# A decoder layer on one core: V's first gathers one per chunk, the zero fill from a small tile and earlier, norm sums and the overflow count later

## The chip, the cores and the metric

The kernel runs on 1 core of one Trainium2 chip (trn2). The metric is the device time of one execution in microseconds (us). The inputs are in the chip's memory before the start, and the kernel is one launch. The engines have separate instruction queues: TensorE (PE in the profile, with its weight loads as PEld), VectorE (DVE), ScalarE (ACT), GpSimd (POOL) and SyncE (SP, which here only issues DMAs). Each queue runs its instructions in order. An instruction that waits holds all that stand behind it on its engine.

## The reference, cut to what matters

One layer of a decoder in float32, for 256 tokens of width 2048, and a last RMSNorm:

```
def hybrid_layer(h, mem, ...):
    hn = rmsnorm(h, norm_mix)
    q_nsa, k_cmp, v_cmp, k_slc, v_slc, k_win, v_win, gate_logits, q_sb, k_sb, v_sb = split(hn @ w_in)
    o_nsa = nsa_attention(q_nsa, ..., t5_table)              # 8 heads, compressed + selected + window
    o_sb = stick_breaking_attention(q_sb, k_sb, v_sb)        # 8 heads
    h = h + concat(o_nsa, o_sb) @ w_out
    h = h + memory_attention(rmsnorm(h, norm_mem_q), rmsnorm(mem, norm_mem_kv), ...)   # 4 heads, 256 memory tokens
    h = h + peer_ffn(rmsnorm(h, norm_ffn), peer_w_q, peer_sub_keys, peer_u, peer_v)
    return h

def peer_ffn(hn, w_pq, sub_keys, u_tab, v_tab):              # per token: 8 heads x 16 experts of 16384
    q = hn @ w_pq                                            # two half queries of 128 per head
    s = q . sub_keys ; top_s, top_i = top_k(s, 16)           # per half: 128 keys, the best 16
    best_s, best_c = top_k(top_s[0] + top_s[1], 16)          # of 256 pairs the best 16
    expert = ia * 128 + ib ; gate = softmax(best_s)
    a = hn . u_tab[expert] ; hidden = gate * gelu(a)
    return sum over the experts of hidden * v_tab[expert]
```

## The kernel before, in words

**Products.** Every float32 product is made of float32r parts. A weight tile of 512 KB (128 x 1024) is loaded by SP into a `raw` buffer (four of them, L60 to L63). ACT copies it into `hi` (L71) and DVE subtracts to get `lo` (L73); there are three buffers of each. A *half block* is one such tile: eight matmuls with `hi` against a pair of activations (L89, 512 columns) and eight with `lo` (L91, 256 columns). Two half blocks make a block of 128 output columns (`fm_block`). `self.last_lo` is always the latest instruction that made a `lo`.

**Stages, in order.** (1) Memory values and keys and the norm of `x`. POOL sums squares (`square_sum`, L183 to L189) into `ssq_m` and `ssq_x`. PE adds these up over the partitions with a matrix of ones (L174 `ps_ssq`, L396 `ps_col`), and ACT and DVE make the reciprocal roots of them (`rstd_rows`, `rstd_columns`). (2) `w_kv`, `w_q`, `w_v`, and four calls of `nsa`, each of which ends with `out_pair` (L578). (3) `w_vsb`, then eight heads of stick-breaking attention; each head makes its `q` and `k` (`qk`), which POOL multiplies by `rstd` (L338). (4) `w_out` in 16 blocks, and memory attention. (5) PEER: 16 blocks of `w_pq`, the two top-16 searches cut into `pieces`, then the *U loop*: all 16384 rows of U as 128 *chunks* of 128 experts, each a block of two half blocks. (6) The *V phase*: rows of V, gathered by expert number, in five calls of `run`. (7) The last norm, in two halves of the tokens.

**The gate table and the lists.** The gates of the chosen experts are scattered into a table in device memory (`by_key`, named `table` in the profile, 16 MB). Lists of the rows of hidden values that aren't zero (`rows`, 12 MB) are written to device memory as well, and read back (`listed`, `index`) for the V phase. Both must be zero before anything is scattered into them. That is the *zero fill*: `clear` (L318) issues one DMA on POOL from a tile of zeros, 128 x 2048 (L311), with a wait on an instruction that it is given: two per stick head on the head's `out_pair`, and one per block of `w_out` on an addition into `hT` (L355).

**V's gathers.** `fetch` (L1029 to L1047) loads a list's indices when they are first needed (L1039) and issues an indirect DMA of 128 rows of V (L1043, 1 MB, rows of 8 KB). Ten of the gathers of the V phase are issued during the U loop, and the other 78 in the V phase. `table_read` (L781) reads a group of the gate table into `hb` during the same loop, and DVE multiplies the activated products by it (L798).

**What sets the order.** The program is written as straight code. A scheduler of the language's own then orders the instructions of each engine by a simulated time line. So code that is written in another place gives the scheduler another priority, and the order of an engine can differ from the order of the code.

Of the kernel before, what the change touches and what calls it, by code (L numbers as in the profile page):

```python
# [18 lines left out]
F32 = mybir.dt.float32  # L19
# [3 lines left out]
SYNC = mybir.DependencyInfo(mybir.DependencyClass.Sync, mybir.DependencyReason.DATA)  # L23
# [29 lines left out]
class Layer:  # L53
# [168 lines left out]
    def front(self):  # L222
        nc, tc, a = self.nc, self.tc, self.a
        with ExitStack() as es:
# [25 lines left out]
            self.rstd_rows(ssq, rstd_m)  # L250
            rstd_mt = fp.tile([128, 2], F32, name="rstd_mt")
            self.rstd_columns(ssq, rstd_mt)
# [4 lines left out]
            ssq = fp.tile([128, T], F32, tag="ssq", name="ssq_x")  # L257
            xT = fp.tile([128, KD, T], F32, tag="big", name="xT")
            for b in range(4):
                xs = xT[:, b * 4:(b + 1) * 4, :]  # L260
                nc.sync.dma_start(xs, a["xT"][:, b * 4:(b + 1) * 4, :])
                p = self.fm_block(a["w_mem_k"][b], pair)
                for n in range(4):
                    k = b * 4 + n
                    self.make_pair(xp, k, xs[:, n, :], self.gs[:, 0, k:k + 1])
                self.join(p, kmT[:, b, :])
                self.square_sum(xs, ssq, b == 0, fp)
# [7 lines left out]
            self.rstd_rows(ssq, rstd)  # L275
            rstd_t = fp.tile([128, 2], F32, name="rstd_t")
            self.rstd_columns(ssq, rstd_t)
            self.qscale = fp.tile([128, 2], F32, name="qscale")
            nc.vector.tensor_scalar_mul(self.qscale, rstd_t, SCALE)
# [4 lines left out]
            for n, name in enumerate(("k_cmp", "v_cmp", "k_slc", "k_win")):  # L284
                kv[name] = fp.tile([128, 2, T], F32, name=name)
                for g in range(2):
                    p = self.fm_block(a["w_kv"][2 * n + g], xp)
                    self.join(p, kv[name][:, g, :])
                    nc.gpsimd.tensor_mul(kv[name][:, g, :], kv[name][:, g, :], rstd)
# [3 lines left out]
            for h in range(8):  # L293
                p = self.fm_block(a["w_q"][h], xp)
                self.join(p, qT[:, h, :])
            turned()
# [8 lines left out]
            for g in range(2):  # L305
                for tb in range(2):
                    self.nsa(g, tb, qT, kv, vt, gates, op)

            v_sb = fp.tile([128, 2, 1024], F32, tag="v_sb", name="v_sb")
            zero = fp.tile([128, 8 * T], F32, tag="qT", name="zero")  # L310
            nc.vector.memset(zero, 0.0)  # L311
            todo = [(self.by_key[:, q * 2048:(q + 1) * 2048], 2048) for q in range(16)]
            for part in range(2):
                for r in range(0, ROWS[part], 7 * 128):
                    n = min(7, (ROWS[part] - r) // 128)
                    todo.append((self.rows[part][r:r + n * 128, :].rearrange("(p n) w -> p (n w)", n=n), n * W))

            def clear(after):  # L318
                if todo:
                    dst, n = todo.pop(0)  # L320
                    ins = nc.gpsimd.dma_start(dst, zero[:, :n])
                    tc.add_manual_dep(ins.ins, after.ins.name, SYNC, reason="not before there is room")
# [9 lines left out]
            for h in range(8):  # L332
# [17 lines left out]
            for b in range(KD):  # L350
# [4 lines left out]
                after = nc.vector.tensor_add(hT[:, b, :], hT[:, b, :], t)  # L355
                clear(after)
# [162 lines left out]
    def nsa(self, g, tb, qT, kv, vt, gates, op):  # L519
# [52 lines left out]
        self.out_pair(op, slice(g * 4, g * 4 + 4), tq, po4)  # L572
# [65 lines left out]
    def peer(self):  # L638
        nc, tc, a = self.nc, self.tc, self.a
        with ExitStack() as es:  # L640
# [16 lines left out]
            with ExitStack() as e2:  # L657
                ps = self.ps = e2.enter_context(tc.tile_pool(name="ups", bufs=2, reuse_waits="tile", space=bass.MemoryType.PSUM))
                pieces = []
                with tc.tile_pool(name="tk", bufs=1, reuse_waits="tile") as tk:  # L660
# [14 lines left out]
                    for h in range(8):  # L675
# [6 lines left out]
                        for p2 in range(2):  # L682
# [15 lines left out]
                            elif 2 * h + p2 in (2, 4, 5, 6, 8, 10, 12):  # L698
                                pieces.pop(0)()
# [30 lines left out]
                while c < 128:  # L730
# [20 lines left out]
                    if part == 1 and not late and len(self.sets) < 10 and c % 3:  # L751
                        self.fetch(len(self.sets))
# [280 lines left out]
    def fetch(self, i):  # L1033
# [9 lines left out]
        nc.gpsimd.indirect_dma_start(  # L1043
# [3 lines left out]
        self.sets[i] = raw  # L1047

    def v_phase(self):
# [6 lines left out]
        with ExitStack() as es:  # L1056
# [99 lines left out]
            with psum("cps") as cps:  # L1156
# [13 lines left out]
                steps.append(excess)  # L1170
# [34 lines left out]
            def finish(tb, q, y):  # L1205
                cs = slice(q * 512, (q + 1) * 512)
                if q == 3:
                    nc.scalar.activation(og[tb][:, cs], og[tb][:, cs], AF.Copy, scale=y)
                else:
                    nc.vector.tensor_scalar_mul(og[tb][:, cs], og[tb][:, cs], y)  # L1210
                nc.sync.dma_start(a["out"][tb * 128:(tb + 1) * 128, cs], og[tb][:, cs])
# [12 lines left out]
            y = root(1)  # L1224
            for q in (3, 0, 1, 2):
                finish(1, q, y)
# [138 lines left out]
```

## Time and profile before

| | |
|---|---|
| three timed runs | 1730.91, 1730.54, 1728.52 us (median 1730.54) |
| the profiled execution | 1733.13 us, of which its span 1731.3 us |
| PE busy | 1649.4 us (95%) |
| DVE, ACT, POOL busy | 1247.5, 983.3, 751.9 us |
| bytes moved by DMA | 414.92 MB, mean 240 GB/s |
| mean granted clock of TensorE | 0.984 |

A row of a time line reads: start in us, us, engine, line, operation, output<-input, shapes, count, and in brackets the idle time before it and what released it. A row of the windows reads: the window, its length, then the busy time of PE, PEld, DVE, ACT and POOL with the number of instructions in brackets, the granted clock of TensorE (1 is full speed), the mean busy share of the 16 DMA engines and the GB/s that they moved. A row of the waits reads: who waited, for whom, us in total, times, the longest.

### The profile page before, as it was taken

To read this page: it belongs to the slowest core of one execution; us is meant where nothing else is said; L and a number is where in the kernel's file an instruction comes from. 1 tells how busy PE (TensorE), PEld (TensorE's weight loads), DVE (VectorE), ACT (ScalarE), POOL (GpSimd) and SP (SyncE) were. 2 spreads that over 40 slices of the span, in tenths; PEclk is the share of its full clock that TensorE was granted. 3 is DMA by queue.
4 is the path that set the end of the run, shared out by engine and by line. 5 is a ranking of instruction groups with operands and counts; after the bars stand their busy time and mean duration, and the time that the engine had idled before them with its cause. 6 is when DMAs were issued, how large, how long until landed. Compare 5 with 4: busy or idle time off the path is not lost. (4 is left out here: it accounts for less than half of the span.)

```text
span 1731.3 us, 25645 instructions
## 1 busy us (share of the span) xinstructions
PE 1649.4 (95%) x8834; PEld 1396.0 (81%) x8834; DVE 1247.5 (72%) x2237; ACT 983.3 (57%) x1457; POOL 751.9 (43%) x651
## 2 busy tenths in 40 slices
PE   7899999999899997999999999999999899999996
PEld 6788787888788876888888888888888677777874
DVE  6935476555568999999984558887665479788687
ACT  6524456675556443666654446665554367567565
POOL 5410000122114378887887720101777117886510
PEclk9999999999999998999999999999999999999998
DMA  7566435689865653565667658886897967998982
GB/s 291 165 218 214 154 98 195 243 313 349 332 220 176 178 164 107 180 194 182 185 192 197 191 187 268 280 291 224 248 272 239 388 232 260 401 408 339 417 326 69
DMA packets 136187, 414.92 MB, mean 240 GB/s; under 512 B 39145, under 2 KB 52073, under 8 KB 122480
## 3 DMA queue, kind: packets, MB, share of 16 engines
q1 hardware_dynamic: 97424, 254.21, 45.3%
q0 software_dynamic: 38624, 158.99, 24.6%
q8 instruction: 71, 1.16, 0.3%
q14 instruction: 68, 0.56, 0.1%
HBM read 369.26 MB, written 49.65 MB: 242 GB/s over the span
## 5 line engine op out<-in xcount | busy, mean ns | idle before, releaser
L73 DVE TENSOR_TENSOR lo<-raw,hi 128x1024 fp32r<-128x1024 f32 x434 | 536.3, 1238 | 282.1 <-ACT hi L71 255.0
L71 ACT ACTIVATE hi<-raw 128x1024 fp32r<-128x1024 f32 x438 | 462.2, 1057 | 427.3 <-PE acc L89 165.1
L89 PE MATMUL acc<-pair_f,hi 128*128 128x512 f32 x2288 | 577.9, 395 | 14.1 <-ACT hi L71 10.0
L89 PEld LDWEIGHTS acc<-pair_f,hi 128*128 128x128 f32 x2288 | 414.2, 190 | 91.7 <-ACT hi L71 12.1
L992 POOL DMA_INDIRECT table<-total,place x256 | 323.9, 1265 | 110.6 <-issue 74.3
L91 PEld LDWEIGHTS acc<-pair_f,lo 128*128 128x128 f32 x2288 | 312.3, 191 | 27.3 <-DVE lo L73 5.6
L91 PE MATMUL acc<-pair_f,lo 128*128 128x256 f32 x2288 | 320.7, 283 | 4.4 <-DVE lo L73 4.4
L876 POOL DMA_INDIRECT rows<-hb,where x128 | 150.0, 1172 | 61.8 <-issue 35.7
L82 DVE SCALAR_TENSOR_TENSOR lo<-vrows,val,hi 128x1024 fp32r<-128x1024 f32 x96 | 122.7, 1282 | 38.9 <-ACT hi L80 33.7
L80 ACT ACTIVATE hi<-vrows,val 128x1024 fp32r<-128x1024 f32 x96 | 109.2, 1148 | 67.6 <-PE out L1071 26.9
L1043 POOL DMA_INDIRECT vrows<-V,index x88 | 116.9, 1328 | 70.3 <-DVE lo L73 22.4
L89 PE MATMUL acc<-pair_x,hi 128*128 128x512 f32 x512 | 131.7, 396 | 0.0
L73 DVE TENSOR_TENSOR lo<-vrows,hi 128x1024 fp32r<-128x1024 f32 x80 | 97.8, 1222 | 17.1 <-PE out L1071 6.7
L89 PEld LDWEIGHTS acc<-pair_x,hi 128*128 128x128 f32 x512 | 91.4, 189 | 17.2 <-issue 1.4
L71 ACT ACTIVATE hi<-vrows 128x1024 fp32r<-128x1024 f32 x80 | 84.3, 1053 | 29.0 <-PE out L1071 20.7
L1071 PE MATMUL out<-hi,ha 128*128 128x512 f32 x256 | 80.7, 407 | 7.3 <-PEq L1238 2.8
L1071 PE MATMUL out<-hi,hb 128*128 128x512 f32 x256 | 82.8, 407 | 2.5 <-issue 1.9
L1071 PE MATMUL out<-lo,ha 128*128 128x512 f32 x256 | 76.3, 401 | 0.4 <-DVE lo L73 0.4
L91 PEld LDWEIGHTS acc<-pair_x,lo 128*128 128x128 f32 x512 | 70.3, 190 | 5.9 <-issue 0.9
L91 PE MATMUL acc<-pair_x,lo 128*128 128x256 f32 x512 | 74.4, 284 | 0.0
L89 PE MATMUL acc<-pair_o,hi 128*128 128x512 f32 x256 | 67.0, 403 | 5.3 <-ACT hi L71 4.4
L1071 PEld LDWEIGHTS out<-hi,ha 128*128 128x128 f32 x256 | 47.5, 191 | 22.2 <-ACT hi L71 6.5
(391 smaller groups left out, 2206.9 us busy)
## 6 DMA issues: line engine op xcount, KB each, us to landing
raw<-U SPq DMA_DIRECT2D x256, 512.0 KB, 4.3
raw<-w_sb SPq DMA_DIRECT2D x32, 512.0 KB, 4.0
table<-zero POOLq DMA_DIRECT2D x16, 1024.0 KB
raw<-w_out SPq DMA_DIRECT2D x32, 512.0 KB, 6.2
raw<-w_pq SPq DMA_DIRECT2D x32, 512.0 KB, 4.1
listed<-rows SPq DMA_DIRECT2D x88, 129.0 KB, 7.3
rows<-zero POOLq DMA_DIRECT2D x12, 903.0 KB
gates<-table POOLq DMA_DIRECT2D x20, 512.0 KB
```

The source lines that it names most:

```text
L71: nc.scalar.activation(hi, raw, AF.Copy)
L73: self.last_lo = (eng or nc.vector).tensor_tensor(out=lo, in0=raw, in1=hi.bitcast(F32), op=ALU.subtract)
L80: nc.scalar.activation(hi, raw, AF.Copy, scale=val)
L82: self.last_lo = nc.vector.scalar_tensor_tensor(lo, raw, val, hi.bitcast(F32), op0=ALU.mult, op1=ALU.subtract)
L89: mm(ps, hi[:, n * m:(n + 1) * m], pair[:, k, :], start=first and n == 0, stop=False)
L91: mm(ps[:, T:], lo[:, n * m:(n + 1) * m], pair[:, k, :T], start=False, stop=last and n == len(ks) - 1)
L876: ins = nc.gpsimd.indirect_dma_start(out=self.rows[part], out_offset=bass.IndirectOffsetOnAxis(ap=where[:, i - lo:i - lo + 1], axis=0), in ...
L992: ins = self.nc.gpsimd.indirect_dma_start(out=self.table, out_offset=bass.IndirectOffsetOnAxis(ap=self.place[tb][:, s:s + 1], axis=0), in_ ...
L1043: nc.gpsimd.indirect_dma_start(out=raw, out_offset=None, in_=self.a["V"], in_offset=bass.IndirectOffsetOnAxis(ap=self.index[part, cls][:, ...
L1071: mm(out[tb][hf * 2 + q], h, v[:, q * 512:(q + 1) * 512], start=first and n == 0, stop=last and n == len(passes) - 1)
```

## The change

- **Zero fill.** The tile of zeros is 128 x 1032 and is cleared early. Each DMA fills the same 1 MB piece of the table as before, now as two runs of 4 KB per partition, and 1 MB pieces of the rows in runs of 4 KB. The 28 DMAs are issued from the queries on: 4 in `w_q`, 3 after each of the four `nsa`, 2 beside `w_vsb`, 1 per stick head, 2 in `w_out`. All but those after `nsa` wait for the latest `lo`.
- **V's first gathers.** They are allowed in every chunk (before: not in each third), and each waits for the latest `lo` of its chunk.
- **Norm sums.** `rstd_rows` and `rstd_columns` for the memory are called behind the first block of `w_mem_k`, and for `x` behind the first block of `w_kv`. `ssq_x` has a buffer of its own.
- **Overflow count.** Two empty steps stand ahead of `excess` in the first `run`.
- **Last norm.** The root and the last scaling of the first half of the tokens become steps of the last `run`.
- **Top-16 pieces.** One place in `w_pq` (2h+p2 = 12) no longer runs a piece, and the first U chunk has none behind it.

```
+                if b == 0:
+                    self.rstd_rows(ssq_m, rstd_m)
+                    self.rstd_columns(ssq_m, rstd_mt)
...
+            zero = fp.tile([128, 4 * W], F32, name="zero")
+            nc.vector.memset(zero, 0.0)
+            todo = [self.by_key[:, q * 2048:(q + 1) * 2048].rearrange("p (a b) -> p a b", b=1024) for q in range(16)]
+            for part in range(2):
+                for r in range(0, ROWS[part], 8 * 128):
+                    n = min(8, (ROWS[part] - r) // 128)
+                    x = self.rows[part][r:r + n * 128, :].rearrange("(p n) w -> p (n w)", n=n)
+                    todo.append(x.rearrange("p (a b) -> p a b", a=2 if n > 4 else 1))
+
+            def clear(n=1, after=None):
+                for _ in range(min(n, len(todo))):
+                    dst = todo.pop(0)
+                    ins = nc.gpsimd.dma_start(dst, zero[:, :dst.shape[2]].unsqueeze(1).to_broadcast(list(dst.shape)))
+                    tc.add_manual_dep(ins.ins, (after or self.last_lo).ins.name, SYNC, reason="not ahead of the loads")
...
+                    if n + g == 0:
+                        norms()
...
+                if h % 2:
+                    clear()
...
-                    self.nsa(g, tb, qT, kv, vt, gates, op)
+                    after = self.nsa(g, tb, qT, kv, vt, gates, op)
+                    clear(3, after)
...
-                after = self.stick(h, qk[0], qk[1], v_sb, sbm, tri, op)
-                for _ in range(2):
-                    clear(after)
+                self.stick(h, qk[0], qk[1], v_sb, sbm, tri, op)
+                clear()
...
-                after = nc.vector.tensor_add(hT[:, b, :], hT[:, b, :], t)
-                clear(after)
+                nc.vector.tensor_add(hT[:, b, :], hT[:, b, :], t)
+                if b % 4 == 3:
+                    clear()
...
-                            elif 2 * h + p2 in (2, 4, 5, 6, 8, 10, 12):
+                            elif 2 * h + p2 in (2, 4, 5, 6, 8, 10):
...
-                        pieces.pop(0)()
+                        if c > 1:
+                            pieces.pop(0)()
...
-                    if part == 1 and not late and len(self.sets) < 10 and c % 3:
-                        self.fetch(len(self.sets))
+                    if part == 1 and not late and len(self.sets) < 10:
+                        ins = self.fetch(len(self.sets))
+                        tc.add_manual_dep(ins.ins, self.last_lo.ins.name, SYNC, reason="beside its chunk")
...
-                steps.append(excess)
+                steps += [lambda: None, lambda: None, excess]
...
-            run(4, steps=[(lambda q=q: square(0, q)) for q in range(4)])
-            for q in range(4):
-                gained(0, q)
-            y = root(0)
-            for q in range(4):
-                finish(0, q, y)
+            ends = [(lambda q=q: [square(0, x) for x in q]) for q in ((0,), (1,), (2, 3))]
+            ends += [lambda: (gained(0, 0), gained(0, 1)), lambda: (gained(0, 2), gained(0, 3))]
+            ends += [lambda: finish(0, root(0))]
+            run(4, steps=ends)
```

**POOL at the end of the U loop**, before. `hb<-table` is a read of the gate table, `index` a load of list indices, `vrows` a gather of V; a wait on DVE is a wait on a `lo` or on the buffer.

```order
L1039 DMA index_14453<-rows_80 128x5x1
L1043 DMA vrows<-V,index_13627 128x2048 [waits DMASW6_49]
L1043 DMA vrows<-V,index_13690 128x2048 [waits DMASW7_49,Pool_49]
L1043 DMA vrows<-V,index_13627 128x2048
L1043 DMA vrows<-V,index_13690 128x2048
L1043 DMA vrows<-V,index_13627 128x2048
L1043 DMA vrows<-V,index_13690 128x2048 [waits DMASW0_49]
L1043 DMA vrows<-V,index_13627 128x2048 [waits DMASW1_49]
L1043 DMA vrows<-V,index_13690 128x2048 [waits DMASW2_49]
L1043 DMA vrows<-V,index_13627 128x2048 [waits DMASW3_49,Activation_49]
L1043 DMA vrows<-V,index_13690 128x2048 [waits DMASW4_49,Activation_49]
L781 DMA hb<-table 128x8x256 [waits DMASW5_49,DVE_49]
```

The same place in the changed kernel:

```order
L794 DMA hb<-table 128x8x256 [waits DMASW4_49,DVE_49]
L1052 DMA index_13732<-rows_80 128x5x1 [waits DMASW5_49,DMASW3_49,DMASW6_49,DMASW2_49,DMASW7_49,DMASW1_49,DMASW0_49]
L1052 DMA index_13788<-rows_80 128x16x1
L1052 DMA index_14369<-rows_80 128x15x1
L1052 DMA index_14375<-rows_80 128x16x1
L1052 DMA index_14451<-rows_80 128x5x1
L1056 DMA vrows<-V,index_13732 128x2048 [waits DMASW5_49,DVE_49]
L1056 DMA vrows<-V,index_13788 128x2048 [waits DMASW6_49,DVE_49,Pool_49]
L1056 DMA vrows<-V,index_13732 128x2048 [waits DMASW4_49,DVE_49]
L1056 DMA vrows<-V,index_13788 128x2048 [waits DVE_49]
```

The table read stands ahead of the indices and gathers now, and each gather waits on DVE.

**POOL from the end of `w_kv` to the stick heads**, before. `table<-zero` and `rows_80<-zero` are the fill, `hT<-xT` is the load of the residual, `qk` the multiplications of stage 3.

```order
L331 DMA tri<-tri 128x128 [waits DMASW2_49,DMASW0_49,PE_49]
L347 DMA hT<-xT 128x1024 [waits DMAHW2_49,DMAHW3_49,DMAHW1_49,DMAHW4_49,DMAHW0_49,DMAHW6_49,DMASW1_49,DMAHW7_49,DVE_49,Activation_49]
L347 DMA hT<-xT 128x1024
L347 DMA hT<-xT 128x1024 [waits DMASW3_49]
L347 DMA hT<-xT 128x1024 [waits DMASW4_49]
L338 TENSOR_TENSOR qk<-qk,rstd 128x256 [waits DVE_49] x4
L338 TENSOR_TENSOR qk<-qk,rstd 128x256 [waits DVE_49,PE_49]
L321 DMA table<-zero 128x2048 [waits DVE_49]
L321 DMA table<-zero 128x2048 [waits DMASW6_49]
```

In the changed kernel:

```order
L296 DMA table<-zero 128x2x1024 [waits DMASW3_49,DVE_49]
L342 DMA tri<-tri 128x128 [waits DMASW4_49,PE_49]
L296 DMA rows_80<-zero 256x1x1032 [waits DVE_49]
L296 DMA table<-zero 128x2x1024 [waits DMASW6_49,DVE_49]
L296 DMA table<-zero 128x2x1024 [waits DMASW7_49]
L296 DMA table<-zero 128x2x1024 [waits DMASW0_49]
L357 DMA hT<-xT 128x1024 [waits DMAHW2_49,DMAHW3_49,DMAHW1_49,DMAHW4_49,DMAHW0_49,DMAHW6_49,DMASW1_49,DMAHW7_49,DVE_49,Activation_49]
L357 DMA hT<-xT 128x1024 [waits DMASW2_49]
L357 DMA hT<-xT 128x1024 [waits DMASW3_49]
L357 DMA hT<-xT 128x1024 [waits DMASW4_49]
L296 DMA rows_80<-zero 256x1x1032 [waits DMASW5_49,DVE_49]
L296 DMA table<-zero 128x2x1024 [waits DMASW6_49,DVE_49]
```

Fill DMAs stand ahead of, and right behind, the loads of `hT`, and among the `qk` further on one per head.

**PE at the norm sum of `x`**, before. `ps_ssq` is the sum over the partitions, `acc` are the half blocks.

```order
L89 MATMUL acc<-pair_x,hi 128x512 x8
L91 MATMUL acc<-pair_x,lo 128x256 x8
L89 MATMUL acc<-pair_x,hi 128x512 x8
L174 MATMUL ps_ssq<-ssq_x,ones 128x256
L91 MATMUL acc<-pair_x,lo 128x256 x8
```

In the changed kernel:

```order
L89 MATMUL acc<-pair_x,hi 128x512 x8
L91 MATMUL acc<-pair_x,lo 128x256 x8
L174 MATMUL ps_ssq<-ssq_x,ones 128x256
L89 MATMUL acc<-pair_x,hi 128x512 x8
L91 MATMUL acc<-pair_x,lo 128x256 x8
```

The sum of `x` stands one group of eight `hi` earlier; the sum of the memory, not shown, stands one half block later than it did.

More of the change, by code (lines that the diff above doesn't have):

```diff
@@ L249, in front @@
             rstd_m = fp.tile([128, T], F32, tag="rstd_m", name="rstd_m")
-            self.rstd_rows(ssq, rstd_m)
             rstd_mt = fp.tile([128, 2], F32, name="rstd_mt")
-            self.rstd_columns(ssq, rstd_mt)
             for tb in range(2):
@@ L256, in front @@
             xp = self.pb.tile([128, KD, 2 * T], F32R, tag="pairb", name="pair_x")
-            ssq = fp.tile([128, T], F32, tag="ssq", name="ssq_x")
+            ssq_m, ssq = ssq, fp.tile([128, T], F32, tag="half", name="ssq_x", bufs=2)
             xT = fp.tile([128, KD, T], F32, tag="big", name="xT")
@@ L274, in front, with norms @@
             rstd = self.rstd
-            self.rstd_rows(ssq, rstd)
             rstd_t = fp.tile([128, 2], F32, name="rstd_t")
-            self.rstd_columns(ssq, rstd_t)
             self.qscale = fp.tile([128, 2], F32, name="qscale")
-            nc.vector.tensor_scalar_mul(self.qscale, rstd_t, SCALE)
+            def norms():
+                self.rstd_rows(ssq, rstd)
+                self.rstd_columns(ssq, rstd_t)
+                nc.vector.tensor_scalar_mul(self.qscale, rstd_t, SCALE)
+            zero = fp.tile([128, 4 * W], F32, name="zero")
[11 more added lines that the diff above has]
+                    tc.add_manual_dep(ins.ins, (after or self.last_lo).ins.name, SYNC, reason="not ahead of the loads")
             consts = [self.compress_consts(n) for n in "kv"]
@@ L306, in front @@
                 for tb in range(2):
-                    self.nsa(g, tb, qT, kv, vt, gates, op)
+                    after = self.nsa(g, tb, qT, kv, vt, gates, op)
+                    clear(3, after)
             v_sb = fp.tile([128, 2, 1024], F32, tag="v_sb", name="v_sb")
[L310 to L322, printed above, removed]
             for cb in range(2):
@@ L354, in front @@
                 nc.vector.tensor_add(hT[:, b, :], hT[:, b, :], p[:, :T])
-                after = nc.vector.tensor_add(hT[:, b, :], hT[:, b, :], t)
-                clear(after)
+                nc.vector.tensor_add(hT[:, b, :], hT[:, b, :], t)
+                if b % 4 == 3:
+                    clear()
                 self.make_pair(hp, b, hT[:, b, :], self.gs[:, 2, b:b + 1])
@@ L571, in nsa @@
         po4 = po.rearrange("p (h t) -> p h t", h=4)
-        self.out_pair(op, slice(g * 4, g * 4 + 4), tq, po4)
+        return self.out_pair(op, slice(g * 4, g * 4 + 4), tq, po4)
     def out_pair(self, op, hs, tq, src):
@@ L1042, in fetch @@
         raw = self.homes[i].tile([128, GROUP * W], F32, tag="hb", name="vrows", bufs=8)[:, :D]
-        nc.gpsimd.indirect_dma_start(
+        ins = nc.gpsimd.indirect_dma_start(
             out=raw, out_offset=None, in_=self.a["V"],
@@ L1047, in fetch @@
         self.sets[i] = raw
+        return ins
     def v_phase(self):
@@ L1203, in root, with finish @@
                 return y
[L1205 to L1211, printed above, removed]
+            def finish(tb, y):
+                for q in (3, 0, 1, 2):
+                    cs = slice(q * 512, (q + 1) * 512)
+                    if q == 3:
+                        nc.scalar.activation(og[tb][:, cs], og[tb][:, cs], AF.Copy, scale=y)
+                    else:
+                        nc.vector.tensor_scalar_mul(og[tb][:, cs], og[tb][:, cs], y)
+                    nc.sync.dma_start(a["out"][tb * 128:(tb + 1) * 128, cs], og[tb][:, cs])
             og = [fin[:, 3, :], fin[:, 0, :]]
             z = [vw.tile([128, 4], F32, tag="fz", name="fz", bufs=2) for _ in range(2)]
-            run(4, steps=[(lambda q=q: square(0, q)) for q in range(4)])
-            for q in range(4):
-                gained(0, q)
-            y = root(0)
-            for q in range(4):
-                finish(0, q, y)
+            ends = [(lambda q=q: [square(0, x) for x in q]) for q in ((0,), (1,), (2, 3))]
+            ends += [lambda: (gained(0, 0), gained(0, 1)), lambda: (gained(0, 2), gained(0, 3))]
+            ends += [lambda: finish(0, root(0))]
+            run(4, steps=ends)
+            assert not ends
             for q in range(4):
@@ L1223, in v_phase @@
                 gained(1, q)
-            y = root(1)
-            for q in (3, 0, 1, 2):
-                finish(1, q, y)
+            finish(1, root(1))
     def rest(self, hidden_pair, products, into):
```

## The prediction

> **What bounds the kernel now.** I read the totals first, then the list of PE's waits, then the time line of PE, DVE and POOL and the windows round the longest waits. The totals:
>
> ```profile
> span 1731.3 us, 25645 instructions
> PE 1649.4 (95%) x8834; PEld 1396.0 (81%) x8834; DVE 1247.5 (72%) x2237; ACT 983.3 (57%) x1457; POOL 751.9 (43%) x651
> ```
>
> PE is the bound: 1649.4 of 1731.3 us, so 82 us are idle. The change takes no matmul away, so it can win only idle time and matmuls at a low clock. Of whom PE waits:
>
> ```profile
> PE acc L89 <- ACT hi L71: 16.4, 13, 2.9
> PE ps_s L904 <- ACT s L907: 10.2, 3, 7.7
> PE acc L91 <- DVE lo L73: 4.4, 3, 2.2
> PE ps_ssq L174 <- POOL ssq_x L189: 3.0, 1, 3.0
> PE ps_over L1161 <- DVE over L870: 2.4, 1, 2.4
> PE ps_ssq L174 <- POOL ssq_m L189: 0.7, 1, 0.7
> ```
>
> The largest wait is for `hi`, a weight tile that came late. I ask where these 16.4 us lie, and what each edit does to them.
>
> **V's first gathers.** A half block on PE, undisturbed and then at the end of the U loop:
>
> ```profile
> 1351.76 1.11 PE L91 MATMUL acc<-pair_f,lo 128*128 128x256 f32 x8
> 1354.56 1.11 PE L91 MATMUL acc<-pair_f,lo 128*128 128x256 f32 x8
> 1356.32 2.12 PE L89 MATMUL acc<-pair_f,hi 128*128 128x512 f32 x8 [0.65 <-ACT hi L71]
> 1361.57 2.11 PE L89 MATMUL acc<-pair_f,hi 128*128 128x512 f32 x8 [2.18 <-ACT hi L71]
> 1365.30 2.11 PE L89 MATMUL acc<-pair_f,hi 128*128 128x512 f32 x8 [0.68 <-ACT hi L71]
> 1369.02 2.11 PE L89 MATMUL acc<-pair_f,hi 128*128 128x512 f32 x8 [0.66 <-ACT hi L71]
> 1372.74 2.11 PE L89 MATMUL acc<-pair_f,hi 128*128 128x512 f32 x8 [0.67 <-ACT hi L71]
> 1376.51 2.11 PE L89 MATMUL acc<-pair_f,hi 128*128 128x512 f32 x8 [0.70 <-ACT hi L71]
> 1379.80 2.11 PE L89 MATMUL acc<-pair_f,hi 128*128 128x512 f32 x8 [0.23 <-ACT hi L71]
> 1384.15 1.51 PE L91 MATMUL acc<-pair_f,lo 128*128 128x256 f32 x8 [2.25 <-DVE lo L73]
> 1385.46 3.31 PE L89 MATMUL acc<-pair_f,hi 128*128 128x512 f32 x8
> 1389.56 2.00 PE L89 MATMUL acc<-pair_f,hi 128*128 128x512 f32 x8
> ```
>
> One half block takes 1354.56 - 1351.76 = 2.80 us and reads 512 KB, so the U loop asks for 187 GB/s. What was in flight, in the windows and on POOL and DVE:
>
> ```profile
> 1336.51 1.08 POOL L1043 DMA_INDIRECT vrows<-V,index  x1 [0.30 <-issue]
> 1349.98 1.00 POOL L1043 DMA_INDIRECT vrows<-V,index  x1 [0.31 <-DMA vrows<-V,index]
> 1350.99 0.95 POOL L781 DMA_DIRECT2D hb<-table  x1
> 1365.30:1376.50 11.20, 9.18 (x48) 7.55 (x48) 5.26 (x8) 4.54 (x8) 0.00 (x0) 1.00 1.02 414
> 1382.54 0.43 DVE L798 TENSOR_TENSOR hb<-hb,ut 128x256 f32<-128x256 f32 x1 [4.83 <-DMA hb<-table]
> ```
>
> All ten gathers (10 MB) are issued from 1336.51 to 1350.98, and the DMA engines are full (1.02, 414 GB/s). The pitch is then 3.72 us (1372.74 - 1369.02), that is 141 GB/s for U: a third of 414. The read of the gate table stands behind the ten, DVE waits 4.83 us for it, and the next `lo` with it. The cost: seven waits of 0.65, 2.18, 0.68, 0.66, 0.67, 0.70, 0.23, sum 5.77 us; 2.25 us behind the table; and two groups at a low clock, 1.51 - 1.11 and 3.31 - 2.00, 1.71 us. Together **9.7 us**. In the new order the table read is ahead, and each gather waits for the `lo` of its chunk, two half blocks apart: 1 MB per 5.6 us, 188 GB/s, with U's 187 makes 375, under 414. While one gather is in flight at the two thirds seen (about 276 GB/s, so 3.8 us) U gets 141 of its 187 GB/s and falls 0.17 MB behind, a third of a tile; in the 1.8 us that remain it gets all 414 and makes it good, and the four tiles loaded ahead cover it. So I take the whole 9.7 back. Bounds: nothing hidden anew, -9.7; every one of 20 half blocks late by the 0.67 seen, +13.4 - 9.7 = +3.7. POOL's wait on `lo` has nothing behind it that is due: the next rows there are gathers, and the first use of them is the V phase at 1412. The index loads stay as they are.
>
> **Zero fill.** In `w_out`:
>
> ```profile
> 436.18 2.11 PE L89 MATMUL acc<-pair_o,hi 128*128 128x512 f32 x8 [1.48 <-ACT hi L71]
> 450.36 3.78 PE L89 MATMUL acc<-pair_o,hi 128*128 128x512 f32 x8 [2.88 <-ACT hi L71]
> 453.94 1.91 PE L91 MATMUL acc<-pair_o,lo 128*128 128x256 f32 x8
> 455.65 2.38 PE L89 MATMUL acc<-pair_o,hi 128*128 128x512 f32 x8
> 430.00:440.00 10.00, 8.52 (x50) 7.32 (x49) 6.08 (x9) 4.36 (x8) 1.10 (x2) 1.00 1.02 423
> 450.00:460.00 10.00, 9.64 (x38) 8.22 (x39) 5.27 (x6) 3.64 (x5) 0.96 (x2) 0.68 0.71 233
> 265.00:290.00 25.00, 25.00 (x121) 18.84 (x120) 15.25 (x37) 17.47 (x41) 2.86 (x5) 1.00 0.71 247
> 300.00:325.00 25.00, 25.00 (x136) 20.14 (x135) 12.68 (x17) 17.07 (x25) 3.34 (x5) 1.00 0.41 130
> 300.00:400.00 100.00, 100.00 (x563) 85.33 (x562) 53.56 (x72) 69.83 (x96) 16.98 (x27) 1.00 0.76 276
> 325.00:350.00 25.00, 25.00 (x144) 21.73 (x143) 13.58 (x20) 18.37 (x25) 5.12 (x8) 1.00 0.93 344
> ```
>
> One DMA of some 1 MB per block fills the engines (1.02, 423 GB/s), a weight tile comes late twice, 1.48 + 2.88 = 4.36 us, and the clock drops behind it: 3.78 - 2.00, 1.91 - 1.11, 2.38 - 2.00, 2.96 us. Together **7.3 us**; with 2 MB left in `w_out` instead of 13, I take all of it. Lower bound of the gain: the clock loss alone stays, 4.4.
>
> A sentence apart: the Trainium skill, "TensorE: Matmul & The Clock Gate" (Part 1), has the clock fall after an idle window of about 3.4 us; here it fell to 0.68 after a wait of 2.88 us, so by the page alone the 2.96 us would not have arisen and the gain would be an estimated 4.4 us. The measured rows decide.
>
> Where do the bytes go? The stick heads drop from 2 MB to 1 MB each, where 276 and even 344 GB/s went with PE never idle (100.00 of 100, 25.00 of 25). The new pressure is at 265 to 330: some 9 MB behind the last three `nsa`, on top of 247 (with `hT`'s 2 MB) and 130 GB/s. On average it fits: 65 us at 414 GB/s are 27 MB, against 6.2 + 5.2 + 10 MB. But 3 MB come at once, and for some 10 us after each `nsa` the engines are full. Bounds: 0 (weights keep their turn), or, with 141 GB/s for weights as at 1365, 11 MB at the other 273 GB/s last 42 us, in which weights that want 163 ((247 x 25 - 2 MB of `hT`) / 25 us) lose 42 x (1 - 141/163) = 5.7 us. I take **+1**, near 0, because four tiles are loaded ahead and the fill comes in three portions with gaps. The memset of the tile lies at DVE's idle start.
>
> Again apart: the Trainium skill, "DMA: Bandwidth & Descriptors" (SWDGE vs HWDGE vs iDMA), says that each DMA engine has internal queues, one kind fed by GpSimd, another by SyncE, and serves them in turn. With rows of 8 KB against U's 4 KB that gives U a third, which agrees with 141 of 414; runs of 4 KB would give weights half, 207 GB/s, more than the 163 wanted, and by the page my +1 would be 0. No trace so far has a fill of 4 KB runs.
>
> **Norm sums.** PE's part of the start:
>
> ```profile
> 48.90 2.66 PE L89 MATMUL acc<-pair_m,hi 128*128 128x512 f32 x8 [2.02 <-ACT hi L71]
> 72.26 0.70 PE L174 MATMUL ps_ssq<-ssq_x,ones 128*128 128x256 f32 x2 [2.98 <-POOL ssq_x L189]
> 44.99 1.28 ACT L163 ACT_TABLE_LOAD   x1
> 68.90 1.65 POOL L269 TENSOR_TENSOR kmT<-kmT,rstd_m 128x256 f32<-128x256 f32 x1 [1.49 <-DVE kmT L125]
> ```
>
> `ssq_m`'s wait (0.7 in the list above) goes, as its sum now stands one half block later. ACT's table load, 1.28 us, leaves its place ahead of the `hi` that PE awaited for 2.02 us: 1.3 goes. ACT's squares, and POOL's rounds of `ssq_x` behind them, come earlier by the same 1.3, and the last addition has two `kmT` ahead of it instead of four, of which the last took 1.65 behind a wait of 1.49; I take 1.2 for that, so the sum is ready 2.5 sooner. But PE is there 0.7 + 1.3 = 2.0 sooner too, so only 0.5 of the 2.98 goes. In all **-2.5**. Bounds: -5 (most of the three waits goes) and +2: the sum stands *eight matmuls earlier* in PE's order, 2.00 us that cover none of POOL's lateness any more.
>
> **The rest.** The overflow count: on PE and DVE its instructions keep their neighbours in the new order, so its 2.4 us stay: 0. The root in `run`: the order of the tail is the same on PE, ACT and DVE: 0. The top-16 piece: PE's order through `w_pq` is the same and DVE gets to the first chunk's `lo` a few instructions sooner: **-0.5** (0 to -1), and the 10.2 us for `ps_s` stay. The V phase gets two writes shuffled: 0 to +1, I take 0.
>
> **Sum.** -9.7 - 7.3 + 1 - 2.5 - 0.5 = -19.0. The profiled execution took 1733.13 us (1.8 more than its span), so 1714.1. It lies 2.6 above the median of the runs shown, 1730.54: on that scale **1711.5 us**, -1.1%. This case's own range: with each term at its best, -9.7 - 7.3 + 0 - 5 - 1 = -23, 1707.5, and 2.4 lower for the spread of the three runs, 1705; with the clock loss in `w_out` staying (+2.9), the fill at 5.7 (+4.7) and no gain at the norm sums (+2.5), 1721.6.
>
> **Rivals.**
> 1. *The fill's stall moves from `w_out` to the `nsa` stage.* For: three portions of 3 MB, and PE at 265 to 330 has weights with no slack when the engines are full. Against: 344 GB/s beside PE at 25.00 of 25. Price: 5.7 us and one spell of low clock, 3.0, in place of the +1: 1711.5 + 7.7 = 1719.
> 2. *Paced gathers delay each half block.* For: U gets only a third while a gather is in flight. Against: four tiles ahead, and 39 GB/s to spare. 20 x 0.67 in place of 0: 1711.5 + 13.4 = 1725.
> 3. *The norm sum of `x` waits longer*, since it stands earlier: +2 in place of -2.5: 1716.
> 4. *Slower: fill DMAs hold POOL's queue.* In front of the `qk` multiplications now stands a DMA that waits for a `lo` and for a free DMA semaphore. If the fill is still draining, `qk` is late, PE's scores are late, once per head. Price per head as at 450: 2.88 wait and 2.96 low clock, 5.8 us, eight heads 47 us: 1711.5 + 47 = 1758. It decides from four heads on (19.0 + 3.5 = 22.5; 22.5 / 5.8 = 3.9). Against:
>
> ```profile
> POOL table L321 <- DVE pair_o L578: 42.1, 7, 8.0
> ```
>
> seven waits of POOL for the head's end, up to 8 us, cost PE nothing between 300 and 400; the new waits are for an earlier instruction.
>
> **How the numbers follow.** A measurement of this kernel can tell 0.2%, 3.5 us, from no change. My forecast has a chance of 0.62, rival 1 0.13, rival 2 0.09, rival 3 0.11, rival 4 0.05. Faster: the forecast, rivals 1 and 3, and some two thirds of rival 2 (1725 is 5.5 under the median, with its own spread) less a little for the forecast's unforeseen: 0.89. Same: 0.06. Slower: 0.05. The range: the forecast's own 1705 to 1722, widened on the upper side to rival 2's 1725, leaves out rival 4, part of rival 2 and the tails of the forecast: 1704 to 1725.
>
> **What would show it.** Right: between the index loads and the V phase PE's time line has no waits for `hi`, and gathers on POOL are 5.6 us apart; in `w_out` DMA share is under 0.9 and the clock 1.00; PE's waits for `hi` fall from 16.4 to about 5. Wrong: waits for `hi` at 265 to 330 (rival 1) or in the gather chunks (2); a wait for `ssq_x` above 3 (3); waits for `qk` in the stick heads (4); or a slower stage that no edit touches.

## The result, and the profile after

The changed kernel takes **1708.47 us** (median; 1707.29 to 1710.42) beside 1730.72 for the kernel before: a ratio of 0.9869, 95% interval 0.9847 to 0.9891. That is 1.3% faster; the forecast was 1711.5 us, with a range of 1704 to 1725. The profiled execution took 1707.29 us, 25.8 less than the one before (1733.13). Its totals and its list of PE's waits:

```profile
span 1705.4 us, 25635 instructions
PE 1640.7 (96%) x8834; PEld 1387.2 (81%) x8834; DVE 1243.1 (73%) x2237; ACT 979.4 (57%) x1457; POOL 760.6 (45%) x649
...
PE ps_s L917 <- ACT s L920: 9.2, 3, 7.1
PE out L1085 <- ACT ha L1095: 4.2, 2, 3.8
PE acc L89 <- ACT hi L71: 2.8, 6, 0.7
PE ps_over L1175 <- DVE over L883: 2.4, 1, 2.4
PE acc L89 <- ACT vm L252: 2.1, 1, 2.1
PE ps_col L407 <- DVE norm_v L176: 0.8, 1, 0.8
```

PE's waits for `hi` fell from 16.4 us in 13 to 2.8 in 6, and both waits for the sums of squares are gone from the list. New are 3.8 us for `ha` where the V phase begins; the wait for `vm` at the start grew from 0.7 to 2.1. PE's busy time fell too, by 8.7 us with the same 8834 matmuls: fewer of them ran at a low clock.

The last matmul comes 25.9 us earlier. Where these lie is read by the same instruction in both time lines; the *lead* is how much earlier it runs in the changed kernel. The start, up to the first matmul of the compressed keys, gives 4.7 us. `w_out` gives 7.8 (its last matmul moved from 490.99 to 478.38, a lead of 12.6 instead of 4.8). The `w_pq` blocks, the top-16 pieces and the U loop up to 1330 us give 1.7. At the end of the U loop the lead goes from 14.2 to 25.6, 11.4 us. From the last U matmul to the first of V 1.5 us are lost again, and the V phase with the tail gains 1.8. The V phase took 301.6 to 310.3 us, from its first to its last matmul, in the fourteen profiles of all kernels here, so these 1.8 us can't be put down to an edit.

**The end of the U loop**, on POOL and then on PE:

```profile
1326.21 0.95 POOL L794 DMA_DIRECT2D hb<-table  x1
1332.38 5.32 POOL L1052 DMA_DIRECT2D index<-rows  x5 [5.22 <-issue]
1338.01 1.08 POOL L1056 DMA_INDIRECT vrows<-V,index  x1 [0.30 <-issue]
...
1347.99 0.99 POOL L1056 DMA_INDIRECT vrows<-V,index  x1 [0.74 <-DVE lo L73]
1355.15 0.99 POOL L1056 DMA_INDIRECT vrows<-V,index  x1 [6.17 <-DVE lo L73]
1362.60 0.99 POOL L1056 DMA_INDIRECT vrows<-V,index  x1 [6.46 <-DVE lo L73]
1370.45 0.99 POOL L1056 DMA_INDIRECT vrows<-V,index  x1 [6.85 <-DVE lo L73]
...
1368.97 2.14 PE L89 MATMUL acc<-pair_f,hi 128*128 128x512 f32 x8 [0.36 <-ACT hi L71]
1372.71 2.10 PE L89 MATMUL acc<-pair_f,hi 128*128 128x512 f32 x8 [0.66 <-ACT hi L71]
1383.41 2.11 PE L89 MATMUL acc<-pair_f,hi 128*128 128x512 f32 x8 [0.22 <-ACT hi L71]
1390.22 2.16 PE L1085 MATMUL out<-hi,ha 128*128 128x512 f32 x4 [3.75 <-ACT ha L1095]
```

The gathers are *not* one per chunk. POOL is held by the index loads until 1337.7, the `lo` of several chunks exist by then, and seven gathers go out in 11 us; only the last three are spaced, 7.2 to 7.9 us apart. Five waits for `hi` are left (0.36, 0.66, 0.68, 0.63, 0.22, sum 2.55 us). There is none at the index loads, where the kernel before waited 0.72 and 2.38.

**`w_out` and the `nsa` stage** in the windows:

```profile
275.00:300.00 25.00, 25.00 (x138) 19.60 (x137) 10.79 (x19) 13.27 (x27) 5.68 (x8) 1.00 1.02 419
430.00:440.00 10.00, 10.00 (x58) 8.72 (x57) 7.21 (x10) 5.55 (x9) 0.25 (x1) 1.00 0.88 297
450.00:460.00 10.00, 10.00 (x61) 8.85 (x60) 6.59 (x10) 4.81 (x7) 0.00 (x0) 1.00 0.61 189
```

In `w_out` the DMA engines have room, and PE works all of the time at full clock. The fill now saturates them for 25 us from 275 on (share 1.02, 419 GB/s), and PE loses nothing there.

**The norm sums**, PE and POOL, and the window of the low clock before and after:

```profile
40.34 2.11 PE L89 MATMUL acc<-pair_m,hi 128*128 128x512 f32 x8 [2.07 <-ACT vm L252]
66.89 0.70 PE L174 MATMUL ps_ssq<-ssq_x,ones 128*128 128x256 f32 x2
65.91 0.92 POOL L189 TENSOR_TENSOR ssq_x<-ssq_x,sq 128x256 f32<-128x256 f32 x1
40.00:60.00 20.00, 18.54 (x98) 14.78 (x99) 18.91 (x29) 17.51 (x30) 11.15 (x10) 1.00 0.54 183
```

```profile
70.50 1.71 POOL L189 TENSOR_TENSOR ssq_x<-ssq_x,sq 128x256 f32<-128x256 f32 x1
40.00:60.00 20.00, 17.58 (x89) 15.16 (x90) 18.80 (x30) 16.86 (x29) 9.35 (x8) 0.91 0.56 187
```

The last addition to `ssq_x` ends at 66.83 instead of 72.21 (second fence: the kernel before), and PE comes to the sum at 66.89 without a wait. Up to the first matmul of the compressed keys PE's idle time fell by 2.6 us and its busy time by 2.1; the clock from 40 to 60 us rose from 0.91 to 1.00.

### The profile page after: what moved, and what is told of

It reads as the page before. It is cut to its first block, busy times and chain, and to the rows that moved or that the text cites. A ratio compares the mean times of both kernels' runs of the same rounds, so it can differ in the third digit from the quotient of the medians.

```text
span 1705.4 us, 25635 instructions
## 1 busy us (share of the span) xinstructions
PE 1640.7 (96%) x8834; PEld 1387.2 (81%) x8834; DVE 1243.1 (73%) x2237; ACT 979.4 (57%) x1457; POOL 760.6 (45%) x649
## 5 line engine op out<-in xcount | busy, mean ns | idle before, releaser
L794 POOL DMA_DIRECT2D gates<-table x20 | 10.7, 535 | 130.1 <-DVE hb L754 73.4
```

The costliest lines, as they stand in the source:

```text
L794: ins = self.nc.gpsimd.dma_start(dst, self.by_key[:, i * T:(i + n) * T].rearrange("j (i t) -> j i t", t=T))
```

## The experiments

Ratios are to the kernel before, run on the same chip in the same call, with their 95% intervals. Intervals of some 4 us each can't tell edits of 2 us apart; for these I use the time lines, by the same instruction in each.

**The gathers alone.** The kernel before with the edit on `fetch` (permission in each chunk, and the wait), and nothing else.

> The kernel before with the edit on V's first gathers alone (one per chunk, each waiting for its chunk's lo). Theory A, my forecast: the ten gathers in a burst starve U's tiles, and spacing takes back the 9.7 us of stalls and low clock from 1356 to 1388: about 1721 us, no wait for hi above 0.3 us behind the index loads. Theory B, from the trace of the change: the gathers are not really spaced there (seven still go out in 11 us), and what went is mainly the pair of waits at the index loads (0.72 and 2.38), where ACT's order has hi behind the next chunk's steps; the order of ACT in this kernel is regular at the index loads but puts two hi behind one another in each of the last chunks: the pair of waits goes, and some waits for hi of 0.3 to 1 us per chunk come in the gather chunks, so 5 to 10 us less, 1721 to 1726.

Measured: 1725.25 us, 0.9958 [0.9939, 0.9976], 7.3 us less by the ratio. Its time line gains 12.7 us between the first score of the top-16 searches and the last U matmul; the pair of waits at the index loads is gone, and the last chunks keep waits of 0.72, 1.03, 0.35 and 0.82 us. Six gathers go out together, then four spaced. So theory B's picture holds, and its size too by the ratio (5 to 10 us); the 12.7 us by the time line are more than either theory had, but this execution had lost 2.1 ahead of that place and loses 2.0 in the V phase, so that its span is 8.6 us shorter.

**The fill alone.** The whole edit on `clear`, its tile and its places, on the kernel before.

> The kernel before with the zero fill's edit alone (28 DMAs of 1 MB from the 4 KB tile, spread from the queries on). Theory A, my forecast: 7.3 us less, about 1723; the two waits in w_out (1.48 and 2.88) and the low clock behind them are gone, and no wait for hi appears from 225 to 330 us, though the DMA engines are full from 275 to 300. Rival 1: the stall only moves to the nsa stage: waits for hi of some 5 us in 265 to 330, 1728 to 1731.

Measured: 1724.28 us, 0.9939 [0.992, 0.9958], 10.6 us less by the ratio; its time line gains 7.9 at the end of `w_out`, without a wait there:

```profile
430.00:440.00 10.00, 10.00 (x61) 8.85 (x60) 6.50 (x10) 5.03 (x7) 0.69 (x1) 1.00 0.79 256
440.00:450.00 10.00, 10.00 (x57) 8.69 (x56) 7.06 (x10) 5.75 (x9) 3.89 (x3) 1.00 0.68 226
```

PE is never idle from 225 to 330 either. Theory A holds; the stall did not move to the `nsa` stage. (The profile's span is only 6.6 us shorter: it loses 4.1 us again from 1107 to 1155, in a part of the U loop that the edit does not touch.)

**The norm sums alone.**

> The kernel before with the norm sums' edit alone. My forecast had 2.5 us less; the trace of the change shows 4.7 us less by the end of the stage, of which 2.7 us are waits and the rest a low clock at 48 to 53 us that no longer comes. Theory A: the whole 4.7 us comes from this edit alone, 1726. Rival: part of it comes from the fill's memset or its other order on POOL and is missing here: 2 to 3 us, 1728.

Measured: 1727.69 us, 0.9962 [0.9942, 0.9982], 6.6 us less by the ratio. Its time line is 4.65 us ahead after the stage, as in the changed kernel (4.67). The edit alone does it. The profile of the kernel before is the fastest of its kind at this place: with the old norm sums the compressed keys start at 111.7 to 114.9 us (six profiles), with the new ones at 107.1 to 107.7 (eight). So the edit is worth 4 to 8 us, 5.7 in the mean. The three ratios multiplied give 0.9860, the whole change has 0.9869: the parts add up within their intervals.

**The size of the runs.** The fill stays at its old places; each DMA is written as two runs of half the length:

```
-                    ins = nc.gpsimd.dma_start(dst, zero[:, :n])
+                    a = 2 if n > 1032 else 1
+                    ins = nc.gpsimd.dma_start(dst.rearrange("p (a b) -> p a b", a=a),
+                                              zero[:, :n // a].unsqueeze(1).to_broadcast([128, a, n // a]))
```

> The kernel before with one thing changed: each fill DMA, at its old place, reads a tile row of at most 4 KB twice instead of 8 KB once, so its runs are 4 KB. Theory A (the place decides: 13 MB in w_out fill the engines): the waits of 1.48 and 2.88 us in w_out stay, 1730. Theory B (the size of the runs decides the share: 4 KB runs of the fill against 4 KB runs of the weights give weights half of 420 GB/s, more than their 187): the waits in w_out are gone without any other place, 1723.

Measured: 1735.16 us, 1.0012 [0.9993, 1.0031]. The waits in `w_out` stay (1.48, 1.03 and 3.14, 5.65 us against 4.36):

```profile
448.31 2.12 PE L89 MATMUL acc<-pair_o,hi 128*128 128x512 f32 x8 [1.03 <-ACT hi L71]
454.51 2.11 PE L89 MATMUL acc<-pair_o,hi 128*128 128x512 f32 x8 [3.14 <-ACT hi L71]
```

This does not decide between the theories, since in `w_out` the packets that the profile counts stayed as long as they were. The sums by queue there show it; q0 is POOL's (the fill), q1 SP's (the weights), and a row reads: packets, MB, share of the time of 16 engines. First the kernel before from 430 to 450 us, then this one from 430 to 456:

```profile
q0 software_dynamic: 697, 4.46, 53.4%
q1 hardware_dynamic: 1036, 3.72, 47.6%
```

```profile
q0 software_dynamic: 861, 5.43, 51.9%
q1 hardware_dynamic: 1136, 4.12, 42.8%
```

4.46 MB in 697 packets are 6400 bytes each, 5.43 MB in 861 are 6300; with runs of 4 KB none could exceed 4128. What is filled there are the lists, and the two halves of a piece were moved together; why is open. Only the pieces of the table, filled earlier, came out shorter: 7270 bytes each before and 3900 here (POOL's queue from 345 to 370), at a place where PE waits in neither kernel. That the waits are gone when the fill is elsewhere is shown by the fill alone; whether shorter packets would have done the same in `w_out`, and whether 8 KB runs would cost something at the new places, was not tried.

**The wait, and the permission in each chunk, apart.** Two kernels: the changed one without the wait, and the kernel before with the wait but its old rhythm:

```
-                        ins = self.fetch(len(self.sets))
-                        tc.add_manual_dep(ins.ins, self.last_lo.ins.name, SYNC, reason="beside its chunk")
+                        self.fetch(len(self.sets))
```

> The changed kernel without the wait on the chunk's lo; a gather may still be issued in each chunk. The table read and the index loads stand where they stand in the changed kernel; ACT's order has hi behind the next chunk's ut and signs again at the index loads. Theory A (spacing of the gathers decides): no waits at the index loads, then a burst of ten in 13 us and 5 to 6 us of waits for hi behind it, none for lo since the table read is ahead: 3 to 4 us over the changed kernel, whose three paced gathers still cost 2.6. Theory B (ACT's order decides at the index loads): the pair of waits, about 3 us, comes back before the first gather is in flight, 6 to 8 us over the changed kernel.

```
                     if part == 1 and not late and len(self.sets) < 10 and c % 3:
-                        self.fetch(len(self.sets))
+                        ins = self.fetch(len(self.sets))
+                        tc.add_manual_dep(ins.ins, self.last_lo.ins.name, SYNC, reason="beside its chunk")
```

> The kernel before with the wait on the chunk's lo alone, the gathers still kept out of each third chunk. ACT's order is regular in all chunks here. Theory A (ACT's order decides at the index loads, the wait only made the scheduler keep it): no pair of waits of 0.72 and 2.38 at the index loads. Theory B (the index loads themselves starve U): the pair stays. For the gathers: two of three chunks have one, so seven or eight go out together behind the index loads and two more are spaced; waits for hi of 1 to 3 us in the last chunks. About 1723, as with the whole edit on the gathers.

Measured: without the wait 1713.33 us, 0.9885 [0.9861, 0.991]; the wait alone on the kernel before 1724.89 us, 0.9953 [0.9931, 0.9974]. The time lines of ACT (and PE in the last rows) at the index loads tell why. First the kernel before:

```profile
1331.58 0.63 ACT L807 ACTIVATE signs<-hb 128x512 bf16<-128x512 f32 x1 [0.49 <-DVE hb L798]
1332.11 1.04 ACT L71 ACTIVATE hi<-raw 128x1024 fp32r<-128x1024 f32 x1
1336.36 0.38 ACT L124 ACTIVATE ut<-acc 128x256 f32<-128x256 f32 x1 [3.21 <-PE acc L91]
1337.55 2.94 ACT L71 ACTIVATE hi<-raw 128x1024 fp32r<-128x1024 f32 x3
1333.21 2.11 PE L89 MATMUL acc<-pair_f,hi 128*128 128x512 f32 x8 [0.72 <-ACT hi L71]
1338.64 2.11 PE L89 MATMUL acc<-pair_f,hi 128*128 128x512 f32 x8 [2.38 <-ACT hi L71]
```

The changed kernel without the wait:

```profile
1330.07 1.04 ACT L71 ACTIVATE hi<-raw 128x1024 fp32r<-128x1024 f32 x1
1331.01 0.62 ACT L819 ACTIVATE signs<-hb 128x512 bf16<-128x512 f32 x1
1334.45 0.38 ACT L124 ACTIVATE ut<-acc 128x256 f32<-128x256 f32 x1 [2.82 <-PE acc L91]
1335.33 0.42 ACT L808 ACTIVATE ut<-ut 128x256 f32<-128x256 f32 x1 [0.49 <-DVE ut L125]
1335.65 2.94 ACT L71 ACTIVATE hi<-raw 128x1024 fp32r<-128x1024 f32 x3
1336.74 2.11 PE L89 MATMUL acc<-pair_f,hi 128*128 128x512 f32 x8 [2.38 <-ACT hi L71]
```

With the wait on the kernel before:

```profile
1333.64 5.36 POOL L1040 DMA_DIRECT2D index<-rows  x5 [4.69 <-DMA rows<-hb,where]
1334.15 1.06 ACT L71 ACTIVATE hi<-raw 128x1024 fp32r<-128x1024 f32 x1 [1.44 <-PE acc L89]
1335.12 0.40 ACT L797 ACTIVATE ut<-ut 128x256 f32<-128x256 f32 x1
1336.95 1.06 ACT L71 ACTIVATE hi<-raw 128x1024 fp32r<-128x1024 f32 x1 [1.43 <-issue]
```

In the first two, `hi` stands behind the finished chunk's `ut`, which waits for PE's accumulation; PE then waits for that `hi`. Three `hi` run in a row (2.94 us) without a wait for a DMA: the tiles had landed. In the third, under the same index loads, `hi` comes every 2.8 us, and PE has no wait from 1160 to the end of the U loop. So the wait of 2.38 is ACT's order, not the DMA: the kernel before, the changed one without the wait and the one with the old gathers (below) have the disturbed order and this wait, and every kernel whose gathers wait for `lo` has neither. The 0.72 is of the same kind in the kernel before (its `hi` stands behind `signs`); without the wait it did not come back. That the scheduler moves `hi` because its own time line sees the burst ahead of U's tiles is my reading of it; no run shows that.

The sizes were off. Without the wait theory B has the cause, but not the 6 to 8 us: the last U matmul is 8.8 us later than in the changed kernel, the whole only 2.6 (by the ratios) to 4.2 (by the spans). With the wait alone four gathers went out together and none of the last chunks waited; seven or eight, and waits of 1 to 3 us, were expected.

The kernel with the wait alone gives some of this back: its V phase begins after a wait of 6.87 us for `ut`, against 2.27 before.

**The old gathers in the changed kernel** (the three lines of the gather edit undone, and with them the two on the top-16 pieces, since ten gathers at the old rhythm need the chunks that these had).

> The changed kernel with V's first gathers and the top-16 places as before (with the old pace of the gathers the earlier places no longer leave room for ten, so the two are undone together). If the gather edit is worth what its part alone showed (11 us between the table of lists and the V phase) also beside the other edits: 10 to 12 us more than the changed kernel, a ratio to before of 0.992 to 0.993, with the burst of ten, the pair of waits of 0.72 and 2.38 at the index loads and 5 to 8 us of waits for hi and lo behind them. Rival (the edits overlap): less than 6 us more.

Measured: 1715.48 us, 0.9901 [0.9871, 0.9931]. Its last U matmul is 8.8 us later than the changed kernel's, the first of V only 6.1, since PE's wait there is shorter (1.03 us).

So the edit is worth some 8.5 us in the U loop and 5.4 (by the ratios) to 7.0 (by the spans) in all; I had expected 10 to 12. Up to the last score of the top-16 searches this kernel and the changed one differ by 0.3 us, all of it from the start: moving those pieces is worth nothing. And its last U matmul ends where the changed kernel without the wait has it (1395.26 and 1395.28 us). So in the U loop the wait is the whole of the gather edit, and the permission in each chunk adds nothing; on the kernel before, the wait alone even brings that matmul 12.8 us forward, and both together 10.6.

**Fewer gathers in the U loop.** The changed kernel with eight from chunk 119 on, and with six from chunk 121 on (the rest at the start of the V phase's code); the edit for six:

```
-                    if part == 1 and not late and len(self.sets) < 10:
+                    if part == 1 and not late and len(self.sets) < 6 and c >= 121:
```

> The changed kernel with eight gathers in the U loop, the first allowed at chunk 119 instead of 117, and the two others at the start of the V phase. Theory A (what is left, 2.6 us of waits for hi at 1369 to 1384, comes from the seven gathers that go out together behind the index loads, a backlog of 7 MB on full DMA engines): five go out together instead of seven, the engines are full for a shorter time, and these waits shrink to under 1 us: 1 to 2.5 us less than the changed kernel in the U loop. Rival: the V phase starts with less in hand and waits the same time for its own rows: no change in the whole.

> The changed kernel with six gathers in the U loop from chunk 121 on, four more at the start of the V phase. Theory A: three go out together, no waits for hi in the last chunks: 2.6 us less there. Rival: the V phase's first products wait for rows (waits of hi on vrows at its start, now 2 waits of 0.4 and 0.7), and lose 2 us or more: no gain, or slower.

Measured: with eight 1712.81 us, 0.9876 [0.9854, 0.9898]; seven still went out together, and the last chunks waited 0.59, 0.65, 0.66 and 0.73 us, as much as in the changed kernel. Theory A's five were not reached, so this run does not test it. With six 1708.25 us, 0.9853 [0.9818, 0.9887]; five went out together (three were expected), and the last chunks had no wait. Beside the changed kernel, on one chip:

> The changed kernel with six gathers in the U loop from chunk 121 on, again, for a comparison with the changed kernel on one chip. Theory A: the 2.6 us of waits for hi in the last chunks are gone and stay gone, 1 to 3 us less than the changed kernel. Rival: its single look ended 0.4 us later than the changed kernel's, so what is won in the last chunks is lost beside them, and the two can't be told apart.

> The changed kernel again, beside the next one on the same chip: a ratio to before of 0.985 to 0.989.

Measured: with six 1705.48 us, 0.9846 [0.9816, 0.9876]; the changed kernel 1709.76 us, 0.987 [0.9846, 0.9893]. There are no waits in the last chunks, and the V phase begins with a wait of 4.60 us, against 3.75 in the changed kernel:

```profile
1391.13 1.22 PE L1085 MATMUL out<-hi,ha 128*128 128x512 f32 x2 [4.60 <-ACT ha L1095]
```

In the first profile of the same kernel that wait was 2.99, so it does not cancel the gain each time. The medians differ by 4.3 us, the intervals overlap widely, and single executions of the two reach from 1702 to 1715. It may be the better kernel; these runs do not settle it.

**The overflow count and the root in `run`, alone.**

> The kernel before with the overflow count two steps later and the root in the last run, nothing else. My forecast: the order of all engines around them is the same, 0 us; the wait of 2.4 us for over stays. Rival: 2.4 us less from the wait, or 1 to 2 us less in the tail.

Measured: 1733.58 us, 0.9998 [0.9979, 1.0016]. Nothing, as forecast. The wait for `over` stays, 3.17 us in its profile and 2.41 in the kernel before.

## Why the prediction was right

- **The bound.** Right: all that was won is PE's idle time and low clock. PE's idle time fell by some 17 us and its busy time by 8.7.
- **The sum, -19.0.** Too small, though the range held the result: the medians differ by 22.3 us and the time lines of the two profiled executions by 25.9. These 6.9 us more are the norm sums (2.2), the V phase (1.8), the end of the U loop (1.7), the stage of the top-16 pieces (1.2), the +1 (1.0) and the fill (0.5), less the 1.5 lost ahead of the V phase.
- **The fill, -7.3, and +1 for the `nsa` stage.** Right in place and size: 7.8 us in `w_out`, 7.9 by this edit alone. The +1 was 0: 25 us of full DMA engines cost PE nothing. Rival 1 fell. The 0 does not show the prediction's half for the weights beside runs of 4 KB; no run tests that share.
- **The gathers, -9.7.** The number held (10.3 us of waits and low clock less: 3.10 + 5.77 + 2.25 + 1.71 = 12.83 before, 2.55 after), by two errors that cancel, which is luck. The step "each gather waits for the `lo` of its chunk, two half blocks apart" failed: POOL comes to the gathers late, and seven go at once; the others are 7.2 to 7.9 us apart, not 5.6, and 2.55 us of waits for `hi` stay. And the sentence "The index loads stay as they are" let the 0.72 and 2.38 beside them stand. They were not the loads' but ACT's order, and went with the wait on `lo`. Rival 2 (each half block late) fell, though the part that stayed is of its kind.
- **The norm sums, -2.5.** Mis-sized: 4.7. The term that was off is "so the sum is ready 2.5 sooner": it was ready 5.4 sooner, since ACT's squares, which POOL's rounds wait for, moved up by 3.6 to 4.6 us, more than the one table load of 1.28. The wait for `vm`, grown from 0.70 to 2.07, took part of that. The other part is the low clock from 40 to 60 us, which I had not counted; it is not the old order's alone, since a profile of the kernel with six gathers has 0.91 there too, behind a wait of 2.85 for `vm`. Rival 3 (a longer wait) fell: the sum eight matmuls earlier waits for nothing.
- **Overflow count and root, 0.** Right, by the run that has them alone. **Top-16 piece, -0.5**: about 0, by the kernel with the old gathers, which undoes it. What the stage gained came without it: from the first `w_pq` matmul to the U loop at 1000 us the changed kernel gains 1.3 us on the kernel before, the fill alone 1.4, the norm sums and the run length alone 1.1, the gathers alone 1.0, the overflow count alone 0. What moves this stage is open.
- **Rival 4, POOL's queue.** Fell: no wait for `qk` from 300 to 400.
- **Not foreseen:** 1.5 us lost where the V phase begins (3.75 us for `ha`, in place of 2.27 for `ut`). PE's first wait there is 1.03 to 2.27 us in the kernels with a burst of ten, and 2.27 to 6.87 where the gathers wait for `lo`. Why is open.

## What to carry to other kernels

When an engine waits for a converted tile, look whether the converter waited for the transfer or for something ahead of it in its own queue: here 3.1 us that looked like late loads were an order, and went when another engine's instruction got a wait. A wait that is meant to space transfers spaces few of them if the issuing engine comes late; count how many go out together. Bulk writes went here to a place where PE's own demand for bytes left room, and the room can be read from the windows in GB/s. A DMA written as shorter runs need not be moved in shorter packets: divide its queue's bytes by its packets before reading anything into the time.

## What the runs showed of the hardware

**Full DMA engines need not hurt.** At 275 to 300 they moved 419 GB/s at a share of 1.02, and PE had no wait. A tile of `w_sb` took 7.3 us from issue to landing (median over the whole of `w_sb`, loaded from some 256 us on), against 4.0 before, and four tiles loaded ahead covered it. The fill's packets there are of 4 KB; behind the gathers, with rows of 8 KB, engines as full (414 GB/s) did cost PE waits; the demand differs too, U's 187 GB/s against the 154 that the weights took here.

**The more gathers go out together, the longer the chunks behind them wait.** With ten in a burst the waits for `hi` behind it summed to 3.3 to 5.8 us (seven profiles), with six or seven to 2.3 to 2.9 (four), with four or five there were none (three). ACT's order differs as well between the first group and the others. In all fourteen, ten gathers are issued before the last U matmul (where the code has eight or six in the U loop, the first of the V phase's go out from 1364 us on), so it is how they are grouped and not how many there are.

**A shorter run in the program is not always a shorter packet.** The lists' pieces, written as two runs of 3.6 KB, went out in packets of 6300 bytes in the mean, where the table's, written as two runs of 4 KB, went out in packets of 3900. What share the weights get beside packets of their own length is read at one place only: in the changed kernel from 275 to 300 the fill moved 6.60 MB in 1707 packets and the weights 3.86 MB in 1070, 37% of the 10.47 MB. PE never waited there, so the weights may not have asked for more. The Trainium skill ("DMA: Bandwidth & Descriptors", SWDGE vs HWDGE vs iDMA) has the engine serve its queues in turn, from which I worked out a half for the weights with equal runs; that stays an estimate, which no run here tests.

**A low clock behind a wait comes and goes.** The same wait of 2.38 us at the same matmuls, first with the fill alone, then with the norm sums alone:

```profile
1333.61 3.69 PE L89 MATMUL acc<-pair_f,hi 128*128 128x512 f32 x8 [2.38 <-ACT hi L71]
```

```profile
1332.23 3.63 PE L89 MATMUL acc<-pair_f,hi 128*128 128x512 f32 x8 [2.38 <-ACT hi L71]
```

In the kernel before these eight matmuls took 2.11 us behind the same wait. In the profile of the gathers alone, whose start is that of the kernel before, the wait for `ssq_x` was 4.51 us instead of 2.98, and the clock fell there instead of at 48 us:

```profile
72.71 1.22 PE L174 MATMUL ps_ssq<-ssq_x,ones 128*128 128x256 f32 x2 [4.51 <-POOL ssq_x L189]
```

There the clock was 0.74 from 72 to 85. So a wait that is removed is worth its length and, in some executions, slow matmuls as well: 1.5 to 1.6 us here (3.63 and 3.69 against 2.11), 2.96 behind the wait of 2.88 in `w_out`. The Trainium skill ("TensorE: Matmul & The Clock Gate", Part 1) calls the clock's window free-running and its effect variable from run to run, which agrees; its 3.4 us of idle time does not, since 2.38 sufficed.
